# A two-level recurrence, shared between GpSimd and VectorE, in a hybrid S5 / pooling / short-convolution trunk

## The chip, the cores and the metric

One core of a Trainium2 chip runs the whole program. The core has engines with a queue of instructions each: TensorE (PE in the profile, PEld its weight loads), VectorE (DVE), ScalarE (ACT), GpSimd (POOL), and SyncE (SP), which only issues DMAs. Each engine takes its own queue in order; between engines an instruction waits on semaphores. The metric is the device time of one execution in microseconds; the median of three runs before is 1680.66 us.

## The reference, cut to what matters

Sequence 1024, model width 1024, two residual layers and a final RMSNorm. The first layer projects the normalized input to four parts, u_a, g_a, u_b, g_b. u_a goes through an S5 mixer (64 groups of 16 channels, 64 complex states per group), u_b through a pooling mixer; both are gated and projected back. The second layer is a gated short convolution.

```python
def s5_mixer(u, ...):                       # cut
    lb_re, lb_im = mag * cos(ang), mag * sin(ang)          # discrete eigenvalues, per group and state
    bu_re = einsum('blgh,gph->blgp', ug, bb_re)            # bu_im likewise
    _, _, s_re, s_im = lax.associative_scan(               # s[l] = lb * s[l-1] + bu[l], complex
        _scan_combine, (a_r, a_i, bu_re, bu_im), axis=1)
    y = einsum('blgp,ghp->blgh', s_re, c_re) - einsum('blgp,ghp->blgh', s_im, c_im)
    y = gelu(y + d_skip * u)
    z = y @ w_glu + b_glu
    return val * sigmoid(gate)                             # val, gate: the halves of z
...
z = h @ ev_w_in[i];  u_a, g_a, u_b, g_b = split(z, 4)
y = concatenate([y_a * silu(g_a), y_b * silu(g_b)])
h_res = h_res + y @ ev_w_out[i]
```

## The kernel before, in words

**Steps and units.** The products run as a list of units, one per step. A full unit is 128 output channels by 1024 tokens: 48 matmuls of 128x512 (float32 in two parts of 12 bits, three products). The order in the first layer is: u_a 0 to 7 (units 0 to 7), g_a 0 and 1 (8, 9), then for each of the four pooling windows two units of u_b, two of g_b, and a half-size pooling unit (10 to 29), then g_a 2 to 7 (30 to 35), then the output projection F_b (36 to 43). In step s (function `steps`) the instructions are issued in this order: the split of unit s+1's weights into an upper part on ScalarE (line 81) and a lower part on VectorE (line 82), the load of unit s+2, the evacuation of unit s-1 (VectorE and ScalarE, in some units through silu or the pooling sums), the step's `pre` work, the matmuls with the step's `mids` spread between them, and the `post` work. Nothing reorders this: what is issued first on an engine runs first there. Upper and lower parts have two buffers each, so that the weights of one unit can be split ahead. A matmul with the lower part stands third in each K tile.

**S5 beside the products.** u_a is stored to DRAM (`ud`) and read back by chunks: token 8c + j of chunk c. In steps 6 to 9 small products turn the 8 tokens of each chunk into the chunk's contribution to the state, W: 128 partitions (two halves of the groups, 64 states each) x 2 (real, imaginary) x 32 columns of groups x 128 chunks, in the slot `big`. `s5_kd` (before step 10's matmuls) stores the convolution kernels K for lags 0 to 7 to DRAM (`kd`, eight DMAs) and builds the matrices `md` from it (eight more). `s5_scan` (lines 419 to 425, issued after step 9) runs the recurrence over the 128 chunks on GpSimd: 127 steps of four 128x64 operations, each on column c of W, at a distance of 128 words between neighbouring elements. `LR` holds the powers 1 to 8 of the eigenvalues; `lreW` and `limW` are the 8th power (real twice, and minus and plus imaginary), the factor from chunk to chunk.

**What needs the scan.** `y_prep(k)` copies the states of 8 groups out of W on ScalarE (line 441), after three GpSimd operations that build the matrix Mo, and then issues the load of u on ScalarE's queue (line 389). `y_work(k)` multiplies: 8 pairs of small matmuls (lines 460 and 461) in each of two pieces. `y_prep(0)` is issued in step 30, `y_work(0)` stands among the matmuls of step 31. The operand C2 (`c2_load`, issued in step 11) has a GpSimd multiplication that stands behind the whole scan.

Of the kernel before, what the change touches and what calls it, by code (L numbers as in the profile page):

```python
# [8 lines left out]
F32 = mybir.dt.float32  # L9
# [6 lines left out]
T = 1024          # tokens, at position j * 128 + c for token 8 * c + j  # L16
D = 1024
NK = D // P       # 8 channel tiles
NG = 64           # S5 groups
NH = 16           # channels of a group  # L20
NJ = 8            # tokens of a chunk
NC = 128          # chunks
# [5 lines left out]
def trunk(ctx: ExitStack, tc: tile.TileContext, a: dict, out: bass.AP):  # L28
# [11 lines left out]
    LD = nc.scalar    # loads in the steps; stores go with S and so never hold a load up  # L40
# [37 lines left out]
    def split_to(h, l, src, scale=None, e=None):  # L78
        # h + l is src * scale, h and l with 12 bits each
        if scale is None:  # L80
            A.activation(h, src, AF.Copy)  # L81
            (e or V).tensor_tensor(out=l, in0=src, in1=h, op=ALU.subtract)  # L82
        else:
            A.activation(h, src, AF.Copy, scale=scale)  # L84
            V.scalar_tensor_tensor(out=l, in0=src, scalar=scale, in1=h, op0=ALU.mult, op1=ALU.subtract)  # L85

# [19 lines left out]
    def mm_k(u, acc, k, first, last, parts, wk=None):  # L106
        # one K tile of a full unit: three products of parts, two token halves
# [9 lines left out]
    def spread(work, n):  # L117
        # hands out the background work of a step over n places
# [15 lines left out]
    # background work by step  # L134
# [6 lines left out]
    def rms_work(sums_of, dst, n):  # L141
        # dst = 1 / sqrt(sum of sums over partitions / D + eps), in two pieces of work
# [43 lines left out]
    # =====================================================================  # L186
    # S5: tables
    # =====================================================================
    con = cp.tile([P, 80], F32, name="con")        # mask (16), inverse counts (64)
# [14 lines left out]
    LR = slot("LR", [P, 2, NG, 8])                 # powers 8 - r of the discrete eigenvalues  # L204
    lreW = cp.tile([P, 2, 32], F32, name="lreW")
    limW = cp.tile([P, 2, 32], F32, name="limW")
    st1 = cp.tile([P, 2, 32], F32, name="st1")
    st2 = cp.tile([P, 2, 32], F32, name="st2")
# [18 lines left out]
    def tt(e, o, x, y, op):  # L227
        e.tensor_tensor(out=o, in0=x, in1=y, op=op)  # L228
# [11 lines left out]
    def exp_ops(e, o, x, w):  # L240
        # o = exp(x), four temporaries w
# [35 lines left out]
    def s5_tables():  # L277
# [49 lines left out]
        # d_skip at lag zero  # L327
# [23 lines left out]
    def z_ic():  # L351
        # identity and, beside it, the output rows of 8 groups
# [4 lines left out]
    def z_build(k):  # L357
        # input matrices of 8 groups, state on partitions
# [12 lines left out]
    def t_work(k):  # L371
        # transposes, and the kernels of lags 0..7 beside them
# [45 lines left out]

    def s5_scan():
        W = s5["W"]  # L420
        for c in range(1, NC):
            tt(G, st1, W[:, :, :, c - 1], lreW, ALU.mult)
            tt(G, st2, W[:, ::-1, :, c - 1], limW, ALU.mult)
            tt(G, W[:, :, :, c], W[:, :, :, c], st1, ALU.add)
            tt(G, W[:, :, :, c], W[:, :, :, c], st2, ALU.add)
# [50 lines left out]
    # =====================================================================  # L476
    # main steps
    # =====================================================================
# [7 lines left out]
    def silu2(g, acc, th=None):  # L486
        # g = 2 * silu(acc * rs); the tanh goes into acc unless th is there
# [15 lines left out]
    def shift_add(o, x, s):  # L503
        # o = x + x shifted by s tokens
# [72 lines left out]
    # the result's rows: the two units' columns; its columns: the two halves of the tokens  # L577
    HB = ("LR", "C1", "B1", "B2", "C2", "t8", "K", "t7")
    H0, H1 = slice(0, 512), slice(512, T)
    # product: operand of the weights, of the activations  # L580
# [25 lines left out]
    class Pair:  # L606
# [37 lines left out]
        def mm(self, i):  # L644
            # neighbours in time lie in different tiles
# [13 lines left out]
        def post(self, i):  # L659
            # adds product i to the results that it is part of; returns work that may come later  # L660
# [29 lines left out]
    # the first two pairs go side by side, as the operands of the activations come in  # L690
# [8 lines left out]
    def run_pairs(pairs, kind, work, pework, tail):  # L699
        # the products of all pairs; work: what else is given to the engines by place  # L700
# [138 lines left out]
    def g_pair(i):  # L839
        def late(g):  # L840
            # t = 2 * t * silu(g)
# [89 lines left out]
    # the last columns, a quarter of the tokens after the other  # L931
# [31 lines left out]
    def j_norm(half, i, c, e):  # L963
        # normalizes columns c of the result's channel tiles 2 i and 2 i + 1
# [64 lines left out]
    for k in range(8):  # L1029
        # transposes of batch k, products of batch k - 1, and what batch k + 2 needs  # L1030
# [6 lines left out]
    at(pre, 10, s5_kd)  # L1037
    at(post, 9, s5_scan)

# [393 lines left out]
```

## Time and profile before

| | |
|---|---|
| median of 3 runs | 1680.66 us (1679.36 to 1684.66) |
| profiled execution, span | 1678.0 us |
| TensorE matmul busy | 1582.0 us (94%) |
| VectorE busy | 1057.9 us (63%) |
| GpSimd busy | 759.8 us (45%) |
| ScalarE busy | 538.8 us (32%) |
| GpSimd scan additions, 128x64, x254 | 122.8 us, mean 483 ns |

The span is the time from the first to the last instruction of one profiled execution; the median lies 2.7 us above it. A line of the timeline gives start, duration, engine, line of the kernel, operation, output<-inputs, shape and count, and in brackets how long the engine stood idle before it and what released it. Neighbouring instructions of one kind are put into one line (x2, x8). A matmul's duration includes its way through the pipeline, so that those of neighbours overlap.

### The profile page before, as it was taken

The page shows a single profiled execution, that of the slowest core. Times are in us where ns is not written, and L with a number is a line of the kernel's source. Part 1 is how long each engine was busy: PE and PEld are TensorE (multiplying, and loading weights), DVE is VectorE, ACT ScalarE, POOL GpSimd, SP SyncE. Part 2 cuts the span into 40 slices and gives each one's busy share as a digit, 9 for nine tenths or more (in the row PEclk, how much of TensorE's full clock was granted, in tenths as well). Part 3 has the DMA queues.
Part 4 walks back from the last instruction along what each step waited for, and adds up shares of the span by engine and source line. Part 5 has one row for each costly group of instructions (what it writes and reads, how often), then busy time and mean ns, then how long its engine had stood idle before and what let it go on. Part 6 is the DMA issues. An engine that isn't in the chain of part 4 may idle for free.

```text
span 1678.0 us, 19261 instructions
## 1 busy us (share of the span) xinstructions
PE 1582.0 (94%) x7186; PEld 1309.3 (78%) x7186; DVE 1057.9 (63%) x1270; ACT 538.8 (32%) x777; POOL 759.8 (45%) x891
## 2 busy tenths in 40 slices
PE   8999999990899999999968999999999999999997
PEld 7788888880788878888846888888888888878886
DVE  5634565650675687673399877768696867763543
ACT  6233121110344343242333332323233332343531
POOL 6952999999632333301346535445353435300001
PEclk9999999995899999999979999999999999999998
DMA  5232532220477732214402212121221212166343
GB/s 208 101 114 91 153 120 70 76 95 17 128 245 237 226 126 101 88 51 149 165 12 60 92 51 76 51 88 63 76 72 54 91 60 76 48 204 204 120 148 117
DMA packets 95036, 181.31 MB, mean 108 GB/s; under 512 B 16352, under 2 KB 52960, under 8 KB 94432
## 3 DMA queue, kind: packets, MB, share of 16 engines
q10 hardware_dynamic: 49664, 116.41, 21.3%
q1 hardware_dynamic: 45280, 63.68, 11.2%
q8 instruction: 57, 0.93, 0.2%
q14 instruction: 35, 0.29, 0.1%
HBM read 141.33 MB, written 42.93 MB: 110 GB/s over the span
## 4 chain that ended last, share of the span: by engine, by line
PE 58%; DVE 5%; DMA 1%; issue 1%; ACT 1%; ACTq 0%; DVEq 0%
PE acc L657 43%; PE acc L904 9%; PE acc L114 4%; PE acc L808 1%; DVE t L228 1%; DVE a L82 1%; DVE ws L82 1%; DVE a L85 1%; PE acc L947 1%; DMA t<-in_glu 0%; DMA hpd<-t 0%; PE aux L168 0%; DVE big L82 0%; ACTq L882 0%; PE aux L150 0%
## 5 line engine op out<-in xcount | busy, mean ns | idle before, releaser
L657 PE MATMUL acc<-a,ws 128*128 128x512 f32 x1920 | 449.2, 389 | 6.4 <-DVE t L228 2.1
L657 PEld LDWEIGHTS acc<-a,ws 128*128 128x128 f32 x1920 | 359.8, 188 | 83.7 <-ACT a L81 3.4
L114 PE MATMUL acc<-a,whi 128*128 128x512 f32 x1440 | 391.7, 394 | 0.2 <-ACT whi L81 0.2
L114 PEld LDWEIGHTS acc<-a,whi 128*128 128x128 f32 x1440 | 268.4, 189 | 55.3 <-issue 1.0
L228 POOL TENSOR_TENSOR t<-t,t 128x512 f32<-128x512 f32 (+2 forms) x81 | 143.7, 1774 | 296.6 <-DVE ws L82 183.6
L82 DVE TENSOR_TENSOR wlo<-raw,whi 128x1024 fp32r<-128x1024 f32 (+2 forms) x89 | 118.2, 1331 | 245.7 <-ACT whi L81 245.4
L657 PE MATMUL acc<-big,ws 128*128 128x512 f32 x960 | 231.2, 396 | 11.3 <-DVE big L82 4.6
L81 ACT ACTIVATE ws<-t 128x512 fp32r<-128x512 f32 x200 | 126.1, 631 | 337.0 <-PE acc L657 198.5
L657 PEld LDWEIGHTS acc<-big,ws 128*128 128x128 f32 x960 | 183.2, 192 | 52.9 <-DVE big L82 5.6
L114 PE MATMUL acc<-a,wlo 128*128 128x512 f32 x720 | 222.1, 390 | 0.0
L82 DVE TENSOR_TENSOR ws<-t,ws 128x512 fp32r<-128x512 f32 x200 | 182.1, 911 | 33.3 <-ACT ws L81 31.4
L114 PEld LDWEIGHTS acc<-a,wlo 128*128 128x128 f32 x720 | 135.4, 188 | 28.5
L904 PE MATMUL acc<-a,whi 128*128 128x512 f32 x480 | 149.9, 393 | 1.5 <-ACT a L84 1.1
L81 ACT ACTIVATE whi<-raw 128x1024 fp32r<-128x1024 f32 (+2 forms) x89 | 86.9, 980 | 193.4 <-PE acc L114 122.9
L228 POOL TENSOR_TENSOR big<-big,st 128x64 f32<-128x64 f32 x254 | 122.8, 483 | 9.9
L228 DVE TENSOR_TENSOR t<-t,acc 128x512 f32<-128x512 f32 x134 | 91.2, 682 | 50.9 <-PE acc L657 50.8
L657 PE MATMUL acc<-td,ws 128*128 128x512 f32 x480 | 117.5, 394 | 0.5 <-DVE td L82 0.5
L904 PEld LDWEIGHTS acc<-a,whi 128*128 128x128 f32 x480 | 90.8, 189 | 21.8 <-ACT a L84 1.5
L657 PEld LDWEIGHTS acc<-td,ws 128*128 128x128 f32 x480 | 91.0, 190 | 21.0 <-issue 1.2
L228 POOL TENSOR_TENSOR t<-t,rs 128x512 f32<-128x512 f32 x5 | 8.7, 1749 | 199.3 <-ACT rs L169 199.3
L904 PE MATMUL acc<-a,wlo 128*128 128x512 f32 x240 | 94.5, 394 | 0.3 <-DVE wlo L82 0.3
L228 POOL TENSOR_TENSOR raw<-raw,raw 128x512 f32<-128x512 f32 x20 | 26.7, 1337 | 121.0 <-DVE ws L82 120.9
(251 smaller groups left out, 1941.8 us busy)
## 6 DMA issues: line engine op xcount, KB each, us to landing
raw<-in_scin ACTq DMA_DIRECT2D x32, 512.0 KB, 4.3
t<-in_scin ACTq DMA_DIRECT2D x32, 512.0 KB, 4.3
raw<-in_scout ACTq DMA_DIRECT2D x32, 512.0 KB, 3.7
raw<-in_win ACTq DMA_DIRECT2D x29, 512.0 KB, 3.6
t<-ud ACTq DMA_DIRECT2D x16, 512.0 KB, 4.4
raw<-in_wout ACTq DMA_DIRECT2D x16, 512.0 KB, 3.6
big<-y2d ACTq DMA_DIRECT2D x15, 512.0 KB, 6.0
ud<-t SPq DMA_DIRECT2D x8, 512.0 KB, 2.6
```

Source lines behind the costliest of these rows:

```text
L81: A.activation(h, src, AF.Copy)
L82: (e or V).tensor_tensor(out=l, in0=src, in1=h, op=ALU.subtract)
L85: V.scalar_tensor_tensor(out=l, in0=src, scalar=scale, in1=h, op0=ALU.mult, op1=ALU.subtract)
L114: PE.matmul(acc[:, n * 512 : n * 512 + 512], lhsT=w, rhs=x[:, n * 512 : n * 512 + 512], start=first and i == 0, stop=last and i == 2)
L228: e.tensor_tensor(out=o, in0=x, in1=y, op=op)
L657: PE.matmul(bank, lhsT=wt, rhs=x[:, k], start=k == 0 and j == 0, stop=k == 3 and j == 2)
L808: PE.matmul(u.acc[:, hs], lhsT=w, rhs=x[:, hs], start=k == 0 and j == 0, stop=k == NK - 1 and j == 2)
L904: PE.matmul(acc[:, 0:512], lhsT=w, rhs=x[:, n % 2], start=n == 0 and i == 0, stop=n == 15 and i == 2)
L947: PE.matmul(acc, lhsT=wt, rhs=x[:, n % 2, quarter(q)], start=n == 0 and i == 0, stop=n == 15 and i == 2)
```

## The change

`s5_kd` moves from before step 10's matmuls to the end of step 9, ahead of the scan. The scan of 128 chunks is split into 16 blocks of 8. Within all blocks at once, item j (1 to 7) adds to column j of each block the factor times column j-1 (`scan_inner`, four operations); then item i (1 to 15) adds to the 8 columns of block i the powers 1 to 8 of the factor times the last column of block i-1 (`scan_outer`, four operations). The powers are built by `scan_powers` on GpSimd into the slot of K, with the slot B1 as a temporary; B1 and B2 also take the products. GpSimd has 12 of the 32 columns of groups, all 22 items at the end of step 9. VectorE has the other 20: its 22 items are handed out among the matmuls of steps 10 to 13, six, six, six and four.

```diff
-    st1 = cp.tile([P, 2, 32], F32, name="st1")
-    st2 = cp.tile([P, 2, 32], F32, name="st2")
...
+    NB = NC // 8
+
+    def scan_tiles():
+        s5["st"] = [slot(f"B{i + 1}", [P, 2, 32, NB]) for i in range(2)]
+        s5["PW"] = slot("K", [P, 2, 2, 32, 8])
+        s5["Wb"] = s5["W"].rearrange("p r g (o j) -> p r g o j", j=8)
+
+    def scan_powers(e):
+        pr, pi = s5["PW"][:, 0], s5["PW"][:, 1]
+        e.tensor_copy(pr[:, :, :, 0], lreW)
+        e.tensor_copy(pi[:, :, :, 0], limW)
+        t = s5["st"][0]
+        for n in (1, 2, 4):
+            lo, up, top = slice(0, n), slice(n, 2 * n), slice(n - 1, n)
+            sh = [P, 2, 32, n]
+            tv = t[:, :, :, 0:n]
+            br, bi = pr[:, :, :, top].to_broadcast(sh), pi[:, :, :, top].to_broadcast(sh)
+            tt(e, tv, pi[:, :, :, lo], bi, ALU.mult)
+            tt(e, pr[:, :, :, up], pr[:, :, :, lo], br, ALU.mult)
+            tt(e, pr[:, :, :, up], pr[:, :, :, up], tv, ALU.subtract)
+            tt(e, tv, pi[:, :, :, lo], br, ALU.mult)
+            tt(e, pi[:, :, :, up], pr[:, :, :, lo], bi, ALU.mult)
+            tt(e, pi[:, :, :, up], pi[:, :, :, up], tv, ALU.add)
+
+    def scan_inner(e, gs, j):
+        n = gs.stop - gs.start
+        sh = [P, 2, n, NB]
+        W, (a1, a2) = s5["Wb"], s5["st"]
+        re, im = (x[:, :, gs].unsqueeze(3).to_broadcast(sh) for x in (lreW, limW))
+        o, q = W[:, :, gs, :, j], W[:, :, gs, :, j - 1]
+        b1, b2 = a1[:, :, gs], a2[:, :, gs]
+        tt(e, b1, q, re, ALU.mult)
+        tt(e, b2, W[:, ::-1, gs, :, j - 1], im, ALU.mult)
+        tt(e, o, o, b1, ALU.add)
+        tt(e, o, o, b2, ALU.add)
+
+    def scan_outer(e, gs, i):
+        n = gs.stop - gs.start
+        sh = [P, 2, n, 8]
+        W, (a1, a2), PW = s5["Wb"], s5["st"], s5["PW"]
+        o = W[:, :, gs, i]
+        b1, b2 = a1[:, :, gs, 0:8], a2[:, :, gs, 0:8]
+        tt(e, b1, PW[:, 0, :, gs], W[:, :, gs, i - 1, 7].unsqueeze(3).to_broadcast(sh), ALU.mult)
+        tt(e, b2, PW[:, 1, :, gs], W[:, ::-1, gs, i - 1, 7].unsqueeze(3).to_broadcast(sh), ALU.mult)
+        tt(e, o, o, b1, ALU.add)
+        tt(e, o, o, b2, ALU.add)
+
     def s5_scan():
-        W = s5["W"]
-        for c in range(1, NC):
-            tt(G, st1, W[:, :, :, c - 1], lreW, ALU.mult)
-            tt(G, st2, W[:, ::-1, :, c - 1], limW, ALU.mult)
-            tt(G, W[:, :, :, c], W[:, :, :, c], st1, ALU.add)
-            tt(G, W[:, :, :, c], W[:, :, :, c], st2, ALU.add)
+
+        scan_tiles()
+        scan_powers(G)
+        for j in range(1, 8):
+            scan_inner(G, slice(0, GP), j)
+        for i in range(1, NB):
+            scan_outer(G, slice(0, GP), i)
+
+    GP = 12
+
+    def scan_work():
+        gs = slice(GP, 32)
+        return [lambda j=j: scan_inner(V, gs, j) for j in range(1, 8)] + [lambda i=i: scan_outer(V, gs, i) for i in range(1, NB)]
...
-    at(pre, 10, s5_kd)
+    at(post, 9, s5_kd)
     at(post, 9, s5_scan)
+    for i, f in enumerate(scan_work()):
+        at_mid(10 + i // 6, [f])
```

VectorE's queue before, from the last copies of W at the end of step 9 (`big` is W) to the split of unit 12 (`wlo`, second of its two):

```order
L404 COPY big_799<-aux_1317 64x512 [waits Activation_49]
L404 COPY big_799<-aux_1324 64x512 [waits Activation_49]
L82 TENSOR_TENSOR wlo_1846<-raw_1201,whi_1845 128x1024 [waits DMAHW3_49,PE_49,Activation_49]
L228 TENSOR_TENSOR t_152_1851<-acc_1208,rs_288 128x1024
L491 SCALAR_TENSOR_TENSOR t_152_1851<-acc_1208,t_152_1851 128x1024 [waits Activation_49]
L412 MEMSET t_153_1856 128x896 [waits DMAHW2_49,DMAHW0_49]
L82 TENSOR_TENSOR wlo_1925<-raw_1849,whi_1924 128x1024 [waits DMAHW6_49,PE_49,Activation_49]
L228 TENSOR_TENSOR t_157_1930<-acc_1875,rs_288 128x1024 [waits DMAHW5_49]
L228 TENSOR_TENSOR t_158_1932<-t_157_1930 128x896 [waits DVE_49,Pool_49]
```

The same place now. Line numbers of the changed kernel are its own: 226 is the helper for a two-operand operation that was 228. Behind the evacuation of unit 9 the queue goes on with the scan; B_151 and B_152 take the products, the names after "waits" are the semaphores of other engines and queues (Pool is GpSimd).

```order
L402 COPY big_797<-aux_1315 64x512 [waits Activation_49]
L402 COPY big_797<-aux_1322 64x512 [waits Activation_49]
L410 MEMSET t_150_1335 128x896 [waits DMAHW2_49,DMAHW0_49]
L82 TENSOR_TENSOR wlo_1466<-raw_1199,whi_1465 128x1024 [waits DMAHW3_49,PE_49,Activation_49]
L226 TENSOR_TENSOR t_156_1471<-acc_1206,rs_286 128x1024
L544 SCALAR_TENSOR_TENSOR t_156_1471<-acc_1206,t_156_1471 128x1024 [waits Activation_49]
L226 TENSOR_TENSOR B_151_1354<-big_797,lreW 128x2x320 [waits Pool_49]
L226 TENSOR_TENSOR B_152_1355<-big_797,limW 128x2x320
L226 TENSOR_TENSOR big_797<-big_797,B_151_1354 128x2x320 [waits DVE_49]
L226 TENSOR_TENSOR big_797<-big_797,B_152_1355 128x2x320 [waits DVE_49]
```

The memset of `s5_kd` has moved ahead of the split of unit 11; where the split of unit 12 stood, the first of 24 scan operations stands, which waits for GpSimd. These are the end of the 24 and what comes after them:

```order
L226 TENSOR_TENSOR B_152_1355<-big_797,limW 128x2x320
L226 TENSOR_TENSOR big_797<-big_797,B_151_1354 128x2x320 [waits DVE_49]
L226 TENSOR_TENSOR big_797<-big_797,B_152_1355 128x2x320 [waits DVE_49]
L82 TENSOR_TENSOR wlo_1550<-raw_1469,whi_1549 128x1024 [waits DMAHW6_49,PE_49,Activation_49]
L226 TENSOR_TENSOR t_160_1555<-acc_1476,rs_286 128x1024 [waits DMAHW5_49]
L226 TENSOR_TENSOR t_161_1557<-t_160_1555 128x896 [waits DVE_49]
L226 TENSOR_TENSOR t_161_1557<-t_160_1555 128x127
L561 COPY t_161_1557<-t_160_1555 128x1
```

The split of unit 12 (`wlo`) now stands behind them, and the evacuation of unit 10 behind that; the splits of units 13, 14 and 15 stand likewise behind 24, 24 and 16 more.

GpSimd's queue before, at the end of step 9 (the last input matrix `t`, then the scan on `big`):

```order
L228 TENSOR_TENSOR t_130_1185<-B_51_653,LR_142 128x896
L228 TENSOR_TENSOR t_129_1184<-t_129_1184,t_130_1185 128x128x7 [waits PE_49,DVE_49,Activation_49,Pool_49]
L228 TENSOR_TENSOR st_145<-big_799,lreW 128x64 [waits DVE_49]
L228 TENSOR_TENSOR st_146<-big_799,limW 128x64
L228 TENSOR_TENSOR big_799<-big_799,st_145 128x64 [waits DMAHW5_49,DMAHW6_49,DMAHW4_49,DMAHW7_49,DMAHW2_49,Pool_49]
L228 TENSOR_TENSOR big_799<-big_799,st_146 128x64 [waits Pool_49]
L228 TENSOR_TENSOR st_145<-big_799,lreW 128x64 [waits Pool_49]
```

And now, from the same place to the fourth operation of the powers (K_1356 is the slot of K, in which the powers come to lie):

```order
L226 TENSOR_TENSOR t_130_1183<-B_51_651,LR_142 128x896
L226 TENSOR_TENSOR t_129_1182<-t_129_1182,t_130_1183 128x128x7 [waits PE_49,DVE_49,Activation_49,Pool_49]
L427 COPY K_1356<-lreW 128x64 [waits DMAHW4_49,DMAHW5_49,DMAHW2_49,DMAHW6_49,DMAHW1_49,DMAHW7_49,DMAHW0_49,DVE_49]
L428 COPY K_1356<-limW 128x64
L226 TENSOR_TENSOR B_151_1354<-K_1356 128x64 [waits Activation_49,Pool_49]
L226 TENSOR_TENSOR K_1356<-K_1356 128x64
L226 TENSOR_TENSOR K_1356<-K_1356,B_151_1354 128x64 [waits Pool_49]
L226 TENSOR_TENSOR B_151_1354<-K_1356 128x64 [waits Pool_49]
```

The first copy into K's slot waits for seven DMA queues (DMAHW), those of the stores out of K; the 18 operations of the powers that follow use B_151, the tile for which VectorE's first scan operation waits.

## Rows read from the trace of the kernel before

**Rows 1.** TensorE's waits, 180 to 560 us: total, times, longest (us).
```profile
PE aux L460 <- DMA t<-ud: 41.3, 1, 41.3
PE aux L461 <- POOL t L228: 5.0, 1, 5.0
```
**Rows 2.** Timeline around step 31's wait: start, us, engine, line, instruction.
```profile
415.60 1.06 ACT L441 ACTIVATE t<-big 64x1024 f32<-64x1024 f32 x1 [52.70 <-POOL big L228]
415.74 0.38 ACTq L389 DMA_DIRECT2D t<-ud  x1
...
418.39 4.79 POOL L228 TENSOR_TENSOR t<-C,LR 128x1024 f32<-128x1024 f32 x2
...
419.89 0.77 PE L460 MATMUL aux<-t,td 128*128 128x128 f32 x2 [41.33 <-DMA t<-ud]
...
423.25 2.35 POOL L228 TENSOR_TENSOR t<-t,t 128x1024 f32<-128x1024 f32 x1
...
425.65 0.79 PE L461 MATMUL aux<-t,t 128*128 128x127 f32 x2 [4.99 <-POOL t L228]
...
428.66 1.69 PE L114 MATMUL acc<-a,whi 128*128 128x512 f32 x4
...
433.39 0.38 PE L460 MATMUL aux<-t,td 128*128 128x128 f32 x2
...
435.09 0.48 PE L114 MATMUL acc<-a,whi 128*128 128x512 f32 x1
```
**Rows 3.** Two stretches: length, then each engine's busy time (instructions), PEclk, DMA.
```profile
core 0: us, PE busy (x) PEld busy (x) DVE busy (x) ACT busy (x) POOL busy (x), PEclk, DMA share, GB/s
172.30:212.00 39.70, 39.70 (x177) 32.88 (x176) 19.22 (x24) 7.02 (x7) 36.56 (x80) 1.00 0.63 161
378.56:428.66 50.10, 3.78 (x18) 3.51 (x17) 4.91 (x3) 6.23 (x6) 46.03 (x106) 0.53 0.13 42
```
**Rows 4.** SyncE's queue ahead of step 31: the stores that free tiles.
```profile
365.60 1.51 SPq L558 DMA_DIRECT2D ybd<-t  x2
```
**Rows 5.** Timeline of VectorE from the end of step 9, and TensorE at unit 15.
```profile
165.69 0.69 DVE L404 COPY big<-aux 64x512 f32<-64x512 f32 x1 [0.20 <-ACT big L406]
...
172.32 0.81 DVE L412 MEMSET t<- 128x896 f32 x1
...
184.80 1.27 DVE L82 TENSOR_TENSOR td<-t,td 128x1024 fp32r<-128x1024 f32 x1 [1.13 <-ACT td L81]
...
210.61 1.41 DVE L82 TENSOR_TENSOR wlo<-raw,whi 128x1024 fp32r<-128x1024 f32 x1 [7.03 <-ACT whi L81]
...
216.11 0.61 PE L114 MATMUL acc<-a,wlo 128*128 128x512 f32 x2
```
**Rows 6.** SyncE's queue: the stores of K and the first of md.
```profile
173.88 8.50 SPq L415 DMA_DIRECT2D kd<-K  x8
185.12 4.23 SPq L417 DMA_DIRECT2D md<-kd  x4
```
**Rows 7.** GpSimd's timeline: the powers LR, first and last of 18, and the one ahead.
```profile
57.76 0.33 POOL L228 TENSOR_TENSOR fri<-td 128x64 f32<-128x64 f32 x1
58.04 0.31 POOL L228 TENSOR_TENSOR td<-LR 128x64 f32<-128x64 f32 x1
...
69.32 1.60 POOL L228 TENSOR_TENSOR LR<-LR,td 128x256 f32<-128x256 f32 x1
```
**Rows 8.** Timeline where VectorE and GpSimd work at once; last VectorE by itself.
```profile
884.62 1.75 POOL L228 TENSOR_TENSOR t<-t,C 128x512 f32<-128x512 f32 x1
...
886.85 3.45 DVE L82 TENSOR_TENSOR a<-B,a 128x512 fp32r<-128x512 f32 x2
...
891.41 1.72 POOL L228 TENSOR_TENSOR t<-t,t 128x512 f32<-128x512 f32 x1
...
1566.20 4.91 DVE L85 SCALAR_TENSOR_TENSOR a<-big,a 128x512 fp32r<-128x512 f32 x8 [0.59 <-ACT a L84]
```
**Rows 9.** Groups by line and shape: busy us, mean ns of one, idle before.
```profile
L228 DVE TENSOR_TENSOR t<-acc,rs 128x1024 f32<-128x1024 f32 x32 | 38.9, 1215 | 11.4 <-DMA ud<-t 8.1 <-ACT rs L169 3.3
L82 DVE TENSOR_TENSOR a<-t,a 128x512 fp32r<-128x512 f32 x8 | 5.2, 682 | 0.0
L366 ACT ACTIVATE t<-B 128x128 f32<-128x128 f32 x8 | 3.6, 447 | 0.0
L368 ACT ACTIVATE td<-C 128x128 f32<-128x128 f32 x8 | 2.7, 334 | 2.2 <-POOL C L232 2.2
```

## The prediction

> **What bounds the kernel now.** I read the busy shares first, then the waits of TensorE, then the stretch around its longest wait in order of time. TensorE is busy 94% of the span, so a change pays only where TensorE stands still. Its waits between 180 and 560 us name one large place: 41.3 us at line 460 for a load of u, with 5.0 us at line 461 behind it [rows 1]. In order of time [rows 2], ScalarE's copy of W (line 441) has stood 52.7 us for GpSimd's last scan addition; the load of u is issued on ScalarE's queue behind that copy (415.74), lands about 4 us later, and only then do the small products of step 31 start (419.89). The load is thus only the last link: the recurrence ends too late. In the stretch from 378.56 to 428.66 TensorE is busy 3.78 of 50.10 us [rows 3].
>
> The second place to read is the one the new work goes to. From 172.30 to 212.00 TensorE is busy all 39.70 us and VectorE 19.22 [rows 3]: there is no slack on TensorE, and VectorE has about 20 us to give, in pieces.
>
> **What the change gives back.** With the scan done early, the stall goes. What stays of it are the 16 small products of one piece, which take 1.70 us at the full clock (433.39 to 435.09, second piece) [rows 2]. Gain: 50.10 - 1.70 = **48.4 us**. What is late next there: the two stores that free the tiles of step 30 are issued by 367.1 [rows 4]; with a landing like that of u (4.2 us, 415.74 to 419.89) u is there by 375.5; GpSimd's three operations for Mo (4.79 for two, then 2.35) [rows 2], from 371.3 on, end near 378.4. Both are just before 378.56, so I count nothing, and up to 2 us against it.
>
> **What it adds before VectorE may start.** Four groups of instructions, 22 items of four, now stand in VectorE's queue in steps 10 to 13, and the weight splits (line 82) of the units 12 to 15 stand behind them in the same queue. An engine takes its queue in order, so each split is as late as all that stands ahead of it. The first scan operation of VectorE waits for GpSimd, because GpSimd's powers use the same B1 tile as a temporary; and GpSimd's first copy waits until the eight stores of K have landed, because the powers lie in K's slot. Priced: VectorE ends its last copy of W at 166.4, the memset (0.81) now follows at once, and the first store of K follows 0.75 us after the memset as before, at 168.0 [rows 5, 6]. From the first store of K to the first md copy, which waits for all eight, it was 11.2 us (173.88 to 185.12) [rows 6], so the slot is free at 179.2. The powers have a twin in the trace: 18 operations of the same 64, 128 and 256 columns, 12.9 us from 58.04 to 70.92 [rows 7]. I take 10.8 us for them and the two copies, since VectorE, which stretched some of those, stands still here (ends: 9 and 13). **VectorE's scan starts at 190.0**; from 172.3 on it does nothing, although it has evacuations and splits to do behind the blocked instruction.
>
> **What VectorE then has to do before the split of unit 15 is through.** Three parts.
> (a) Its old work of this stretch: 19.22 us, less the memset 0.81, plus three waits of 1.13 inside evacuations for ScalarE's answer [rows 3, 5]: 21.8 us.
> (b) Its scan operations. At the full rate eight operations of 512 columns take 4.91 us, 0.61 each; the slope between 512 and 1024 columns (0.682 and 1.215 us) is 1.04 ns per column [rows 8, 9]. The 28 inner operations have 640 columns: 0.61 + 128 x 1.04 ns = 0.74 us, 20.8 us together. The 60 outer ones have 320: 0.41 us, 24.5 us. That is 45.4 us. The inner operations read and write every eighth word of a row, which no VectorE instruction of before does. Below: nothing more. Above, by the nearest rows: ScalarE's 128x128 copy that writes every eighth word took 447 ns, against 334 ns for one of the same size into runs of 16 words [rows 9], 0.88 ns more per column; on 640 columns 0.56 us, on 28 operations 15.8 us. I take the upper of these two, because it is a price measured on this very access step: (b) is 61.2 us.
> The Trainium skill, "Vector Engine (DVE) Microarchitecture Reference", section 5.2 (Measured stream behaviour on trn2), speaks against the change here too: a port runs at the full rate only over runs of at least two adjacent words, and its table has 1.7 to 2.5 ns per column instead of 1.05 for single words. By it the inner operations would take 1.2 to 1.7 us and the total would be 2 to 10 us above mine; no VectorE row of before shows it.
> (c) The turns with GpSimd, which runs its own share at the same time. Where both engines had a row of 512-column operations on SBUF, neither ran beside the other: GpSimd started one every 1.70 us (884.62 to 891.41, four), and VectorE's took 1.73 [rows 8]. So 1.70 = 0.61 (VectorE) + 1.09 (GpSimd): each waits out the other. GpSimd's hold is 2.13 ns per column, 0.82 us for its 28 inner operations of 384 columns and 0.41 for the 60 outer ones of 192: 47.6 us. Some of it falls into VectorE's reads of PSUM and its waits in (a); I take **40 us** (ends 30 and 48).
>
> The sum: 190.0 + 21.8 + 61.2 + 40 = 313.0, when the lower part of unit 15's weights is ready. Before, TensorE took it up at 216.11, right behind the products before it [rows 5]. So TensorE is **96.9 us late** there. I expect it in pieces: about 50 us at unit 12 (behind six inner items and the start at 190), some 15 to 20 each at units 13 and 14, 10 or less at 15. Behind unit 15 no scan item is left on VectorE; the scan is then complete, and needed near 420 at the earliest. After the last long wait the clock costs a little: granted 0.5 of full speed (1.2 GHz) when work came back in before, the 16 small products took 3.0 us (425.65 to 428.66) instead of 1.7 [rows 2]; I add 2 us.
>
> Net: 96.9 + 2 - 48.4 = +50.5. The profiled execution has a span of 1678.0 us, the median of the runs is 1680.66; what lies around the span (2.7) does not change. **1680.7 + 50.5 = 1731 us.**
>
> The part that costs nothing: the store of sgad 96 now stands behind K's stores and the md copies on SP's queue; nobody reads it for hundreds of us, and its tile is next written by unit 11's evacuation, which comes behind the blocked scan. The md copies come about 6 us earlier and are first read in step 30.
>
> **Rivals.**
> A. Single words at a step of eight cost VectorE nothing: (b) is 45.4, total 1715 us. For it: GpSimd's operations on LR, same step, are as short as those on packed rows (0.31 at 58.04, 0.33 at 57.76) [rows 7]. Against it: the ScalarE rows.
> B. The step costs more: once for the reading of a multiplication, and twice, reading and writing, in an addition: 14 x 0.56 = 7.9 us more, 1739 us; with GpSimd's inner operations dearer by half as well (28 x 0.41 = 11.5), 1750. The latter is a rule of the Trainium skill, "GPSIMD Engine Reference", section 7 (Performance pitfalls for Q7 kernels): reads with a step over 8 bytes cost about half more. The LR operations do not show it.
> C. The engines do not take turns in these operations. Then (c) is nothing, the operations run at their lone durations (0.07 more each, 6 us), the total is 1697 us; and at full rate as well 1681 us, not slower than before. This one mechanism decides the sign: the change breaks even when VectorE's whole scan, turns included, takes 50 us or less. Against it are the rows 8; for it, only that these were operations with other operands.
> D. VectorE isn't held up at its first scan operation (the wait is met already at 172), and C at full rate holds: 18 us less, 1664 us. This is the change as it would look if the recurrence fitted beside the steps. Against it: 45.4 us of bare work do not fit into 20 us of idle time, so TensorE waits some 23 us even then.
>
> **How the numbers follow.** Forecast 0.60 (1731; its own range, from the ends of powers and turns, 1719 to 1741). A 0.17, B 0.11, C 0.06 (half of it at each price), D 0.06 (with the mixtures of it and A that end well below the time before). The range of 1696 to 1758 leaves out the low half of C, D, and some 0.05 above, where the upper ends of several terms add up. A measurement of this kernel can tell 0.3% (5 us) from no change. Faster: D, 0.06; same: C at full rate, 0.03; slower: the rest, 0.91.
>
> **What will show it.** In the waits of TensorE: none at line 460 of over 2 us in step 31, and at the weight products (line 114 of before) four new waits for VectorE's lower parts, together 90 to 100 us, the first the longest. In VectorE's timeline: nothing from about 172 until 190, released by GpSimd. In the groups: inner operations of VectorE at 128x640 near 2.1 us on average beside GpSimd (1.3 bare), outer ones near 0.8; those of GpSimd stretched likewise. GpSimd's and VectorE's scan over by about 315. If VectorE's operations are no longer beside GpSimd's than alone, (c) is wrong; if VectorE's first scan operation starts right behind the evacuation at 172, the hold-up is; if TensorE still waits at step 31, the gain is.

## The result and the profile after

Median 1730.93 us (four runs, 1728.78 to 1731.63) against 1680.47: ratio 1.0292, 95% interval 1.0279 to 1.0305, slower. The forecast was 1731. The profiled execution has a span of 1727.0 us, 49.0 more than before.

TensorE's waits from 160 to 600 us in the changed kernel (engine, line, released by: total, times, longest):

```profile
PE acc L114 <- DVE wlo L82: 81.9, 3, 48.8
PE acc L114 <- DVE t L226: 5.7, 1, 5.7
PE aux L513 <- DMA td<-md: 1.3, 1, 1.3
```

The 41 and 5 us of [rows 1] are gone; line 513 is what was 460. In their place stand four waits for VectorE, here in TensorE's timeline, at the units 12, 13, 14 and 15 (three for the lower part of the weights, `wlo`, the last for an evacuation, `t`):

```profile
238.82 1.22 PE L114 MATMUL acc<-a,wlo 128*128 128x512 f32 x2 [48.78 <-DVE wlo L82]
...
271.43 1.22 PE L114 MATMUL acc<-a,wlo 128*128 128x512 f32 x2 [19.43 <-DVE wlo L82]
...
298.97 1.22 PE L114 MATMUL acc<-td,wlo 128*128 128x512 f32 x2 [13.66 <-DVE wlo L82]
...
312.11 2.05 PE L114 MATMUL acc<-a,whi 128*128 128x512 f32 x4 [5.71 <-DVE t L226]
```

The two operations of VectorE that end the last of them, the split of unit 15 and the evacuation of unit 13:

```profile
309.62 1.22 DVE L82 TENSOR_TENSOR wlo<-raw,whi 128x1024 fp32r<-128x1024 f32 x1
310.75 1.22 DVE L226 TENSOR_TENSOR t<-acc,rs 128x1024 f32<-128x1024 f32 x1
```

The chain that leads there, from SyncE's stores through GpSimd's powers to VectorE's first scan operation (compare [rows 5 to 7]):

```profile
169.14 6.72 SPq L413 DMA_DIRECT2D kd<-K  x8
...
178.91 0.31 POOL L427 COPY K<-lreW 128x64 f32<-128x64 f32 x1 [31.16 <-DMA kd<-K]
...
188.71 0.73 POOL L226 TENSOR_TENSOR K<-K,B 128x256 f32<-128x256 f32 x1
...
189.48 1.32 DVE L226 TENSOR_TENSOR B<-big,lreW 128x640 f32<-128x640 f32 x1 [16.38 <-POOL K L226]
190.72 2.01 DVE L226 TENSOR_TENSOR B<-big,limW 128x640 f32<-128x640 f32 x1
192.65 4.17 DVE L226 TENSOR_TENSOR big<-big,B 128x640 f32<-128x640 f32 x2
```

VectorE does nothing for 16.4 us, then runs one operation of 1.3 us and from there on operations of 2.0: the first started 0.04 us before GpSimd's (189.52) and was not held up, the next ones take turns with GpSimd's. Two stretches, in the form of [rows 3]:

```profile
172.30:200.00 27.70, 17.74 (x79) 14.36 (x77) 11.26 (x7) 1.06 (x1) 19.91 (x26) 0.92 0.87 225
200.00:300.00 100.00, 28.09 (x99) 22.16 (x100) 96.40 (x87) 3.59 (x4) 95.96 (x84) 0.62 0.03 8
```

Between 200 and 300 us VectorE and GpSimd are both busy 96% and TensorE 28%. Part of that busy time is waiting for one another: VectorE's scan operations take 96.1 us in the changed kernel (sum of their groups) and 65.3 without GpSimd's share (e4, below), so the profile counts an operation that waits for its turn as busy.

### The profile page after: what moved, and what is told of

It is laid out like the page before. It is cut to its first block, busy times and chain, and to the rows that moved or that the text cites. A ratio compares the mean times of both kernels' runs of the same rounds, so it can differ in the third digit from the quotient of the medians.

```text
span 1727.0 us, 18952 instructions
## 1 busy us (share of the span) xinstructions
PE 1591.1 (92%) x7186; PEld 1313.7 (76%) x7186; DVE 1143.9 (66%) x1358; ACT 537.4 (31%) x777; POOL 644.1 (37%) x491
## 4 chain that ended last, share of the span: by engine, by line
PE 75%; DVE 12%; POOL 5%; issue 3%; DMA 2%; SPq 1%; ACT 1%; ACTq 0%; DVEq 0%; POOLq 0%
PE acc L710 42%; PE acc L114 20%; PE acc L957 9%; DVE B L226 3%; DVE big L226 3%; DVE t L226 2%; POOL td L226 1%; PE acc L861 1%; POOL td L230 1%; PE aux L378 1%; DVE wlo L82 1%; PE aux L396 1%; DVE a L85 1%; PE aux L513 1%; PE aux L514 1%
## 5 line engine op out<-in xcount | busy, mean ns | idle before, releaser
L226 POOL TENSOR_TENSOR t<-C,LR 128x1024 f32<-128x1024 f32 (+1 forms) x18 | 34.4, 1913 | 263.7 <-DVE t L609 167.4
L226 DVE TENSOR_TENSOR t<-t,acc 128x512 f32<-128x512 f32 x134 | 91.2, 681 | 50.6 <-PE acc L710 50.5
L81 ACT ACTIVATE ws<-raw 128x512 fp32r<-128x512 f32 x80 | 50.0, 626 | 73.7 <-PE acc L710 51.6
```

## The experiments

Each was run beside the kernel before on the same chip. Where a run is called faster or slower, the interval of its ratio to the kernel before lies wholly on that side of 1; of the differences, only those of the changed kernel, e3, e5 (just) and e12 reach 2%. The runs e4, e5, e8 and e12 leave out or change part of the recurrence and are there only for what they tell of the time. "Theory" and "rival" are the two outcomes that each expectation names.

| run | median, us | ratio to before (95%) |
|---|---|---|
| changed kernel | 1730.9 | 1.0292 (1.0279 to 1.0305) |
| e1 GpSimd alone | 1681.5 | 0.9986 (0.9976 to 0.9995) |
| e2 spread | 1683.0 | 1.0004 (0.9994 to 1.0013) |
| e3 own temporary | 1720.1 | 1.0217 (1.0202 to 1.0232) |
| e4 no GpSimd share | 1696.6 | 1.0080 (1.0064 to 1.0095) |
| e5 inner packed | 1715.8 | 1.0201 (1.0186 to 1.0216) |
| e6 by chunks | 1670.2 | 0.9932 (0.9917 to 0.9946) |
| e8 spread, no GpSimd share | 1652.5 | 0.9827 (0.9810 to 0.9845) |
| e9 VectorE alone, spread | 1680.7 | 0.9997 (0.9987 to 1.0008) |
| e10 by chunks, store first | 1658.1 | 0.9864 (0.9847 to 0.9880) |
| e11 even | 1665.1 | 0.9902 (0.9887 to 0.9917) |
| e12 no scan | 1631.7 | 0.9702 (0.9688 to 0.9717) |
| e13 by chunks, seven blocks | 1658.6 | 0.9864 (0.9845 to 0.9882) |

**The gain by itself (e12).** The kernel before without its recurrence:

```diff
-    at(post, 9, s5_scan)
```

> The kernel before with its recurrence left out altogether (the states are not carried from chunk to chunk). What it tells is the size of the gain term by itself. Theory (the wait at step 31 hangs on the scan alone, and what is late next is just before it): 1630 to 1635 us. Rival (the load of u or the matrix Mo takes the wait's place in part): 1638 to 1650 us.

1631.67 us, 48.9 less than before (forecast of the term: 48.4). No wait at line 460 of over 2 us is left:

```profile
PE aux L460 <- DMA td<-md: 1.5, 1, 1.5
```

So the whole wait at step 31 hung on the scan, and nothing took its place.

**The turns (e4).** GpSimd's share left out of the changed kernel:

```diff
         scan_powers(G)
-        for j in range(1, 8):
-            scan_inner(G, slice(0, GP), j)
-        for i in range(1, NB):
-            scan_outer(G, slice(0, GP), i)
```

> GpSimd builds the powers but leaves out its share of the scan (12 of 32 columns are not computed); VectorE's share stands as in the changed kernel. Theory (turns cost 40 us): inner operations of VectorE take about 1.3 us instead of 2.0, outer ones 0.47 instead of 0.77, TensorE's last wait ends near 275 us instead of 312: 1690 to 1697 us. Rival (the operations take 2 us because of their strided access and not because of GpSimd): 1728 to 1731 us.

As the theory had it. The groups of the changed kernel, VectorE's two largest, and after them the same groups of this run, the group with the hold-up, and TensorE's last wait (in a group: count, busy us, mean ns of one, idle before):

```profile
L226 DVE TENSOR_TENSOR big<-big,B 128x640 f32<-128x640 f32 x14 | 27.9, 1991 | 0.2
...
L226 DVE TENSOR_TENSOR big<-big,B 128x320 f32<-128x320 f32 x30 | 21.6, 720 | 0.5
```

```profile
L226 DVE TENSOR_TENSOR big<-big,B 128x640 f32<-128x640 f32 x14 | 18.5, 1319 | 0.2
L226 DVE TENSOR_TENSOR big<-big,B 128x320 f32<-128x320 f32 x30 | 14.6, 488 | 0.5
...
L226 DVE TENSOR_TENSOR B<-big,lreW 128x640 f32<-128x640 f32 x7 | 9.7, 1391 | 17.1 <-POOL K L226 16.9
...
276.62 2.04 PE L114 MATMUL acc<-a,whi 128*128 128x512 f32 x4 [6.05 <-DVE t L226]
```

The same instructions of VectorE take 1.32 us instead of 1.99. TensorE's last wait ends at 276.62 instead of 312.11: the turns are 35.5 us of the loss. The hold-up of 17 us stays, as it should.

**The step of eight words (e5).** The inner items on columns that lie side by side:

```diff
-        W, (a1, a2) = s5["Wb"], s5["st"]
+        W, (a1, a2) = s5["W"].rearrange("p r g (j o) -> p r g o j", j=8), s5["st"]
```

> The inner items, on both engines, read and write columns of W that lie side by side (16 chunks in a row) instead of every eighth word; number, size and order of the operations stay, the recurrence then runs over the wrong chunks. Theory (VectorE pays some 0.5 us for the step of eight words in each of its 28 inner operations): an inner operation of VectorE and its turn fall from 2.0 to about 1.5 us, total 1715 to 1720 us. Rival (the step costs nothing, the 2.0 us are turns alone): 1728 to 1731 us.

The theory again. The groups of the inner additions, GpSimd's and then VectorE's (2.00 and 1.99 us in the changed kernel):

```profile
L226 POOL TENSOR_TENSOR big<-big,B 128x384 f32<-128x384 f32 x14 | 21.0, 1500 | 0.5
...
L226 DVE TENSOR_TENSOR big<-big,B 128x640 f32<-128x640 f32 x14 | 20.0, 1432 | 0.2
```

The last wait ends at 298.63, 13.5 us earlier, 0.48 us for each of 28 operations. Both engines' operations became shorter by the same half microsecond, since in turns a saving of one is a saving of both; the run doesn't tell alone whose price it was. e4 does: beside no GpSimd work, 1.32 us for 640 columns is 0.58 more than the 0.74 of the packed rate; with 0.07 for the start of a lone operation, 0.5 us of step. That is all that e5 saves, so in the turns no price of GpSimd's for the step shows (alone it has one, see e1).

**The hold-up (e3).** The temporary of the powers in another slot:

```diff
-        t = s5["st"][0]
+        t = slot("C2", [P, 2, 32, NB])
```

> The temporary of the powers lies in the slot of C2 instead of B1, so that VectorE's first scan operation does not wait for the powers. Theory (17 us of the loss are VectorE standing still from 173 to 189.5): VectorE's scan starts at 173, its end and TensorE's last wait come 14 to 17 us earlier: 1713 to 1718 us. Rival (VectorE's start does not count, since GpSimd's turns set the pace until its own end near 296 us): 1726 to 1731 us.

Less than expected: VectorE's scan starts at 174.7 (14.8 us earlier), but TensorE's last wait ends at 302.05, 10.1 earlier, and the run is 11 us faster (13 by the ratios):

```profile
174.72 1.35 DVE L226 TENSOR_TENSOR B<-big,lreW 128x640 f32<-128x640 f32 x1
...
302.05 2.05 PE L114 MATMUL acc<-a,whi 128*128 128x512 f32 x4 [12.63 <-DVE t L226]
```

The rest was given back at once, because GpSimd's powers now ran beside VectorE. One of the 64-column operations that took 0.3 to 0.4 us in the changed kernel:

```profile
184.20 1.48 POOL L226 TENSOR_TENSOR K<-K 128x64 f32<-128x64 f32 x1
```

GpSimd's first inner operation came at 209.2 instead of 189.5, and its share ended at 299.7 instead of 296.2.

**Where VectorE's work stands (e2).** The 22 items over 15 steps:

```diff
+    free = [s for s in range(11, 29) if s not in (14, 19, 24)]
...
-        at_mid(10 + i // 6, [f])
+        at_mid(free[i * len(free) // 22], [f])
```

> The same instructions as in the changed kernel, 20 columns on VectorE, but its 22 items are handed out one or two to a step over 15 of the steps 11 to 28 instead of six to a step in 10 to 13. Theory (the loss is that the items stand in front of weight splits in a bunch that does not fit between them): no wait of TensorE above 2 us between 170 and 560 us, the gain of 48 us at step 31 is kept: 1632 to 1640 us. Rival (VectorE's additional 64 us of work and 40 us of turns cost the same wherever they stand): 1700 to 1731 us.

Neither theory nor rival. 48 us came back against the changed kernel, but TensorE still waited 40.2 us:

```profile
PE acc L114 <- DVE wlo L82: 21.5, 4, 10.1
PE acc L114 <- DVE t L226: 18.7, 2, 13.8
```

So nothing was won against before. A stretch in the form of [rows 3]:

```profile
200.00:280.00 80.00, 48.05 (x181) 38.23 (x180) 73.42 (x52) 8.59 (x9) 77.65 (x59) 0.79 0.17 59
```

VectorE is busy 73.4 of 80 us. The theory took for granted, without a sum, that the work fits between the splits once it is spread. e8 asks which part does not fit.

**Spread, without GpSimd's share (e8).** e2 and the edit of e4 together.

> As the spread version (VectorE's 22 items over 15 of the steps 11 to 28), but GpSimd leaves its share of the scan out (12 of 32 columns are not computed). Theory (the 40 us that the spread version still loses are turns with GpSimd between 190 and 255 us): VectorE's old work of 120 us and its new 64 us, with some 18 us of waits for ScalarE, fit into the 206 us: waits of TensorE of 8 us or less, 1632 to 1642 us. Rival (VectorE's own scan work does not fit between the splits, with or without turns): 1665 to 1683 us.

1652.5: between theory and rival. GpSimd's share costs 30 of e2's 40 us, as turns. What is left are two waits (4.8 and 10.6 us) between 200 and 236 us, where the spread by number still puts two of the dear inner items into one step, behind a hold-up of VectorE of 5.9 us at its first scan operation.

**All on GpSimd (e1).** `GP = 32`, and VectorE's items not handed out.

> GpSimd has all 32 columns of the two-level scan, VectorE none; the rest is as in the changed kernel. Theory (splits queued behind VectorE's scan, and turns between the two engines): VectorE isn't blocked at 172 us, no wait of 49 us at unit 12; but GpSimd's 28 inner operations of 1024 columns hold VectorE up for some 2.2 us each and the 60 outer ones for 1.1, so that VectorE's splits come 10 to 40 us late in all between 190 and 340 us, and the scan ends between 370 and 395 us: 1650 to 1685 us. Rival (only the work given to VectorE counts, there are no turns): no wait at the splits, 1633 to 1642 us.

In the theory's range, at its slow end, and within 0.3% of the kernel before. VectorE has no scan work here and yet is late. TensorE's waits between 160 and 600 us add up to 36.5 us for weights and evacuations, most of them for ScalarE's upper parts, because ScalarE's queue in its turn stands behind a result of VectorE (25.76 us before 216.35). One line of the waits, then stretches of VectorE's and GpSimd's timelines:

```profile
PE acc L114 <- ACT whi L81: 25.5, 4, 7.5
```

```profile
194.88 2.62 POOL L226 TENSOR_TENSOR B<-big,lreW 128x1024 f32<-128x1024 f32 x1
...
200.00 6.29 POOL L226 TENSOR_TENSOR big<-big,B 128x1024 f32<-128x1024 f32 x2
...
203.80 1.22 DVE L226 TENSOR_TENSOR t<-acc,rs 128x1024 f32<-128x1024 f32 x1 [11.90 <-DMA sgad<-t]
205.06 4.80 DVE L226 TENSOR_TENSOR t<-t 128x896 f32<-128x896 f32 x2
...
213.40 2.70 DVE L226 TENSOR_TENSOR t<-t,con 128x16 f32<-128x16 f32 x1
```

An operation of 16 columns that took 0.22 us before takes 2.70 beside GpSimd's of 1024 columns, while one that reads PSUM (1.22) is as short as ever. VectorE's first row is another thing: a wait of 11.9 us for the store of sgad 96. While VectorE stood there, GpSimd had its inner operations to itself: 2.62 us for a multiplication and 3.1 for an addition, against 1.17 and 1.30 for its outer ones of half the columns, where these ran alone. Measured by twice those (2.34 and 2.60), GpSimd pays an eighth to a fifth more for the step of eight words.

**All on VectorE (e9).** `GP = 0`, spread as in e2, the powers with the temporary of e3, GpSimd's items left out because it has no columns.

> All 32 columns of groups on VectorE (operations of 1024 and 512 columns), its 22 items over 15 of the steps 11 to 28, GpSimd only builds the powers, with a temporary of its own. Theory (port time counts: a column costs 2.1 ns on GpSimd and 1.0 to 1.8 on VectorE, so no turns and less time in all): about 90 us of scan beside 120 of old work and 18 of waits, 15 to 25 us more than the stretch has: 1645 to 1660 us. Rival (as much is lost as with the sharing): 1675 to 1690 us.

As the rival had it. With GpSimd's share, and so its turns, gone, TensorE waits 36.0 us (27.6 of it for evacuations), and the run is level with the kernel before. The stretch from 172 to 360 us of this run, and of e12, which has no recurrence:

```profile
172.00:360.00 188.00, 155.10 (x635) 125.81 (x634) 159.26 (x164) 25.89 (x28) 29.74 (x21) 0.90 0.27 78
```

```profile
172.00:360.00 188.00, 188.00 (x832) 155.65 (x831) 105.29 (x140) 34.13 (x34) 2.78 (x1) 1.00 0.33 98
```

Without a recurrence VectorE has 82.7 us to spare here (188.0 - 105.3), many of them short gaps; its scan operations take 100.3 us (sum of their groups).

**By chunks (e6).** GpSimd runs the first 63 steps as before (`scan_one`, the four 64-column operations); the last 64 chunks go in two levels, their inner operations (`ops`) one by one over VectorE's steps 11 to 23:

```diff
+    HB0, HB1 = 8, 12
...
+        for c in range(1, 8 * HB0):
+            if c == 24:
+                scan_powers(G)
+            scan_one(G, c)
...
+    ops = [f for j in range(1, 8) for f in scan_inner(V, j)]
...
+    at(post, 23, lambda: [scan_outer(G, i) for i in range(HB0, HB1)])
...
+        at_mid(27 + (i - HB1) // 2, [lambda i=i: scan_outer(V, i)])
```

> The recurrence is shared by chunks instead of columns: GpSimd runs the first 63 steps one after the other as in the kernel before (64-column operations, short turns), VectorE meanwhile the inner items of the last 8 blocks (28 operations of 512 columns, spread over steps 11 to 23), then GpSimd the outer items of blocks 8 to 11 and VectorE those of 12 to 15 (steps 27, 28); powers with a temporary of their own. Theory (short GpSimd operations hold VectorE up little, and VectorE has only about 28 + 20 us of new work): waits of TensorE of 10 us or less between 170 and 560 us, scan complete by 362: 1632 to 1645 us. Rival (any new work on VectorE or GpSimd there costs as much as the wait at step 31 gives): 1670 to 1690 us.

1670.2, faster than before by 0.7%, but neither theory nor rival. Two places were not foreseen. GpSimd's steps took 2.6 us on average, against 1.64 where VectorE stood idle, so that its part ended at 382.8 and VectorE waited for it. And VectorE stood still once more for the store of sgad 96:

```profile
204.58 1.23 DVE L226 TENSOR_TENSOR t<-acc,rs 128x1024 f32<-128x1024 f32 x1 [10.77 <-DMA sgad<-t]
```

On SyncE's queue that store was issued at 197.48, behind eight stores of K and eight md copies.

**The store first (e10).** As e6, with `s5_kd` again at the head of step 10, behind that store, and the powers behind it. Two things moved with it: the zero tile of `s5_kd` lies in another slot, and the two temporaries of GpSimd's steps (`t`) are packed, where e6 has them at a step of eight words.

```diff
-    at(post, 9, s5_kd)
...
+    at(pre, 10, lambda: (s5_kd(), s5_scan2()))
...
-        b1, b2 = (x[:, :, :, 0] for x in s5["sg"])
+        b1, b2 = s5["s1"]
```

> The version shared by chunks, but with the stores of K again before step 10's matmuls, behind the store of g_a 1 (sgad 96), so that VectorE no longer stands still 10.8 us at 193.8 us for that store; the powers and the later GpSimd steps follow them. Theory (that wait is what made TensorE wait 5 us at 216 and 225 us): those waits go, the late ones at 374 to 400 us stay: 1662 to 1667 us. Rival (VectorE catches up anyway, the early wait costs nothing): 1668 to 1672 us.

1658.1, more than expected: the early waits are gone, and GpSimd's part ends at 369.5 instead of 382.8 (5.3 us of that are its earlier start, since its temporaries' slot no longer waits for a store). The rest fits the packed temporaries: a pair of GpSimd's additions without VectorE beside it, first in e6 and then in this run, is 0.13 us shorter, 8 us for the 63 pairs. So e10 tells the two changes together, not the order of the store alone.

```profile
178.76 0.95 POOL L226 TENSOR_TENSOR big<-big,t 128x64 f32<-128x64 f32 x2
...
178.64 0.82 POOL L226 TENSOR_TENSOR big<-big,t 128x64 f32<-128x64 f32 x2
```

These waits stay:

```profile
365.49 1.56 PE L114 MATMUL acc<-td,whi 128*128 128x512 f32 x4 [3.93 <-ACT whi L81]
...
375.46 1.22 PE L114 MATMUL acc<-td,wlo 128*128 128x512 f32 x2 [8.41 <-DVE wlo L82]
...
386.49 1.93 PE L114 MATMUL acc<-a,whi 128*128 128x512 f32 x4 [4.17 <-DVE t L226]
```

**The border moved by a block (e13).** e10 with `HB0, HB1 = 7, 10`; VectorE's inner operations end in step 21.

> The last version shared by chunks, with the border moved by one block: GpSimd runs 55 steps instead of 63 and the outer items of three blocks instead of four, VectorE the inner items of nine blocks (steps 11 to 21) and six outer items (three each in steps 27 and 28). Theory (in the version before it TensorE waited 17 us at 365 to 387 us because GpSimd ended at 369 and VectorE stood behind it): GpSimd ends near 345, VectorE doesn't wait for it, half of the 17 us go: 1648 to 1655 us. Rival (the sum of work in the stretch is what counts, wherever the border is): 1656 to 1661 us.

As the rival had it: GpSimd ends at 346.7 and VectorE no longer waits for it, but with six outer items before the splits of steps 27 and 28 TensorE waits anew; 1658.6. The border isn't what limits.

```profile
371.92 1.22 PE L114 MATMUL acc<-td,wlo 128*128 128x512 f32 x2 [7.96 <-DVE wlo L82]
...
385.61 2.04 PE L114 MATMUL acc<-a,whi 128*128 128x512 f32 x4 [6.43 <-DVE t L226]
```

**The change in another order (e11).** The shares and operations of the changed kernel; GpSimd's inner items ahead of its powers, which have the temporary of e3, `s5_kd` back in step 10, VectorE's items spread by cost over 16 steps:

```diff
+    free = [s for s in range(10, 29) if s not in (14, 19, 24)]
+    cost = [2.7] * 7 + [1.0] * 15
```

> Shares of 12 and 20 columns and all operations as in the changed kernel, only the order differs: GpSimd's inner items first and its powers after them, with a temporary of their own; the stores of K back before step 10's matmuls; VectorE's 22 items handed out evenly by their cost over 16 of the steps 10 to 28. Theory (order and hold-ups are about half of what the spread version lost, VectorE's work and turns the rest): 1658 to 1668 us. Rival (VectorE's total, with 47 us of turns, is too much for the stretch whatever the order): 1678 to 1686 us.

1665.1, as the theory had it: 17 us better than e2 (the ratios differ by 1.0%), 66 better than the changed kernel, and faster than before. The operations and their engines are those of the changed kernel; order, places and the slot of the temporary differ, and no run separates these three.

## Why the prediction was right

Step by step, as the prediction had it, with what the profile of the changed kernel or a run gave:

| step | predicted | measured |
|---|---|---|
| gain at step 31 | 48.4 | 48.9 (e12) |
| K's slot free, GpSimd's first copy | 179.2 | 178.91 |
| powers and two copies | 10.8 | 10.5 (178.91 to 189.44) |
| VectorE's scan starts | 190.0 | 189.48 |
| (b) VectorE's scan operations, alone | 61.2, or 67 as lone ones | 65.3 (e4) |
| of it for the step of eight words | 15.8 | 13.5 (e5) |
| (c) turns | 40 | 35.5 (e4) |
| split of unit 15 ends | 313.0 | 310.84 |
| TensorE goes on at unit 15 | 313.0 | 312.11 |
| clock behind the last wait | 2 | 3.0 |
| net change of the span | +50.5 | +49.0 (of the medians: +50.5) |

The mechanism was the one forecast, with its four waits (about 50, 15 to 20 twice, up to 10; measured 48.8, 19.4, 13.7, 5.7). Some details differ. The start of the powers came out by two errors that cancel: the first store of K came 1.1 us later than forecast (169.14, not 168.0), and the eight landed in 9.7 us instead of 11.2 (md's first copy at 178.82). The last wait was not for the lower part of the weights but for the evacuation right behind it (line 226, t, 310.75 to 311.97): the accumulator of unit 15 was the one that unit 13 had held, a wait that the prediction had not looked for and that costs a microsecond. The prices of the step of eight words and of the turns were 17 and 13% too high; and VectorE's old work was too low, by the same turns: from 189.48 to 310.84 are 121.4 us, of which the scan operations are 96.1 (sum of their groups), which leaves 25.3 for the old work against 21.8. Turns that the prediction put into (c) stand in part in (a). These differences cancel, so the agreement within 1 us is in part luck; by these errors a sum of this kind is good to some 5 us (an estimate).

The clock is the term that came out larger: unit 15 starts 96.9 us late (312.11 against 215.21 before), its fourth K tile 99.9 us late (319.16 against 219.28), at a clock near half of full speed in between (granted 0.54):

```profile
312.11:318.70 6.59, 6.59 (x17) 5.16 (x18) 4.75 (x4) 1.95 (x2) 0.00 (x0) 0.54 0.46 152
```

At the second piece of step 31 TensorE is 50.8 us late (484.18 against 433.39). By the end of the span 49.0 are left: some 2 us differ behind 850 us, where the change has no instruction, and why is not shown. The medians differ by 50.5.

The rivals: A (no price for the step) fell with e5, C (no turns) with e4. D's place, the hold-up, is real but worth 10 to 13 us, not 18 (e3). Of B's dearer prices the first is not seen: in e4 VectorE's additions (1.32 us) are no dearer than its multiplications (1.30 and 1.39). The second is seen at less than half its size where GpSimd runs alone (e1: an eighth to a fifth, not half), and not in the turns (e5). One figure of the prediction doesn't follow: 28 operations at 1.2 to 1.7 us are 34 to 48 us against the 36.6 of its own sum, which is from 3 us below its total to 11 above, not 2 to 10 above.

What the prediction passed over: it called the move of the sgad store behind K's stores harmless because the blocked scan covers it. That held in the changed kernel. Where the scan was not blocked (e1, e6), the same move held VectorE up by 11.9 and 10.8 us. It had named the cover and not what it costs without it.

The prediction also didn't say what would be left if the bunch in steps 10 to 13 were undone. e2 and e9 show it: the two-level recurrence has more columns than the one-level one (28 x 1024 + 60 x 512 = 59392 over its operations against 508 x 64 = 32512), and whether GpSimd or VectorE has them, they end up on VectorE's time, as work (e9) or as turns (e1). Of the kernels with the whole recurrence, e6, e10, e11 and e13 came out ahead, the best of them, e10 and e13, 1.4% faster than before; none came near the 1632 us of e12. VectorE's total by itself is not the limit. The stretch from unit 10 to step 31, 213.8 us long before, in e2, e11 and e9, in the form of [rows 3]:

```profile
167.31:432.81 265.50, 225.32 (x947) 183.55 (x946) 210.84 (x238) 41.53 (x43) 134.34 (x114) 0.92 0.28 85
...
167.22:413.07 245.85, 222.17 (x947) 181.84 (x946) 209.28 (x239) 42.96 (x45) 141.51 (x114) 0.96 0.31 93
...
166.38:429.60 263.22, 227.19 (x947) 184.96 (x946) 215.69 (x239) 43.07 (x45) 40.58 (x26) 0.92 0.29 87
```

VectorE's busy time, waiting for turns included, is 210.8, 209.3 and 215.7 us: only e9's is longer than the 213.8, and e2 and e11, 1.5 us apart in it, are 20 us apart in length. Where the work stands and what holds it up count as well as how much it is; how each loss divides between them was not tried, for instance with old work of VectorE taken away.

## What to carry to other kernels

Before work is moved to an engine that is "63% busy", read its timeline for the stretch where the work goes: how much is idle there, what stands behind the new instructions in its queue, and who waits for that; here 65 us of work, before its turns, in front of four weight splits with 20 us of slack cost more than the 48 us that it took away elsewhere. Price VectorE and GpSimd, where both work on SBUF as in these rows, as the sum of their times, not the longer one. And when an instruction is moved ahead of a store, look for the buffer which that store frees.

## What the runs showed of the hardware

VectorE and GpSimd, both busy with operations on SBUF, waited for each other instruction by instruction. Four rows of the changed kernel, in order of time, two engines:

```profile
196.85 1.95 DVE L226 TENSOR_TENSOR B<-big,lreW 128x640 f32<-128x640 f32 x1
...
197.81 1.84 POOL L226 TENSOR_TENSOR B<-big,lreW 128x384 f32<-128x384 f32 x1
...
198.73 2.00 DVE L226 TENSOR_TENSOR B<-big,limW 128x640 f32<-128x640 f32 x1
...
199.60 1.97 POOL L226 TENSOR_TENSOR B<-big,limW 128x384 f32<-128x384 f32 x1
```

Each record starts about where the engine's own last one ended and lasts a whole pair of turns. New against [rows 8] is that a short operation can pay nearly the other's full length: 2.70 us for 16 columns in e1, 1.48 for 64 columns on GpSimd in e3. It depends on when it comes: of ten VectorE operations of 16 columns beside GpSimd's scan in e1, four took 0.18 us, three 1.1 and three 2.3 to 2.7. On VectorE, 640 columns at a step of eight words took 1.32 us alone; less 0.07 for the start that is 1.95 ns per column (and 1024 columns took 2.16 us in e9, a slope of 2.2), against a slope of 1.04 for packed ones [rows 9]. The table of the Trainium skill, "Vector Engine (DVE) Microarchitecture Reference", section 5.2 (Measured stream behaviour on trn2), with 1.7 to 2.5 ns per column for single words, agrees with that.
